# Feed-forward input products as seven half-size products for eight, with weight sums on GpSimd

## The chip, the cores and the metric
One core of a Trainium2 chip runs the whole program in one launch. The metric is the device time in microseconds (us), the median of repeated runs. TensorE multiplies; VectorE (DVE in the rows), ScalarE (ACT) and GpSimd (POOL) do the elementwise work; SyncE (SP) issues the transfers from HBM. Each engine works through its own queue in order, and waits at an instruction whose input is not there.

## The reference
A trunk of two layers on a sequence of 512 tokens with 1024 features, in float32. Each layer has a mixer (layer 0: HGRN2 and stick-breaking heads, layer 1: mLSTM heads) and a feed-forward part, both conditioned on a vector c. The feed-forward part is what the change touches:
```
def modulate(x, g, shift, scale):
    return (rmsnorm(x, g) * (1.0 + scale) + shift)

def conv_glu_ffn(h, w_in, conv_w, conv_b, w_out):
    u = jnp.matmul(h, w_in)                 # 512 x 1024 by 1024 x 5632
    a, g = jnp.split(u, 2, axis=-1)         # 2816 features each
    a = causal_dwconv(a, conv_w, conv_b)    # 3 taps along the tokens
    return jnp.matmul(jax.nn.gelu(a) * g, w_out)

x = x + g_f * conv_glu_ffn(modulate(x, norm_ffn_g, sh_f, sc_f), ...)
```
The six shifts, scales and gates of a layer come from `silu(c) @ ada_w + ada_b`, a vector of 6144 per layer.

## The kernel before
Activations are held with features on the 128 partitions and tokens along the row: a tile is 128 features by 512 tokens. Products run in a three-term form: every operand is split into a rounded part (hi) and its rest (lo), and `mm3` (L188) issues hi·hi, lo·hi and hi·lo.

The feed-forward input has 22 tiles of `a` and 22 of `g`. Two tiles of each make a pair of tiles (`fi` is the first tile's number). For a pair, `load_split` (L166) fetches 1024 rows by 256 columns of the `a` weights and as much of the `g` weights into raw buffers of 2048 per partition; ScalarE casts them to hi (L177), VectorE subtracts to lo (L178). `mms` (L1001) then runs 8 x 3 products of 512 columns per tile, 96 a pair. As soon as a tile of `a` is in PSUM, `act_a` (L985) makes the convolution: ScalarE the newest tap with the bias (L988), VectorE two more (L990, L992). When the tile of `g` is there too, `act_g` (L996) takes gelu on ScalarE (L997), multiplies by `g` (L998) and splits into `acth` (L184) and `actl` (L185) on VectorE. The first pair of a layer, `first_half` (L1005), runs in two halves of the tokens, since the second half of h comes later.

Output products: tiles are taken in groups of 8, 8 and 6; behind each of the first two groups 4 blocks of output weights are multiplied with the group's activations and added to x (L314), the third goes through `halves_out` (L316), one token half after the other, which also prepares the next norm.

Conditioning runs beside it: `ada_chunk` (L118) fetches 512 KB of `ada_w` into one of three `ada` buffers four times and accumulates 8 products on VectorE (L129, L131), and `ada_close` (L140) transposes on TensorE, reduces (L147) and adds (L149). A *step* is one fetch with its two products. `take` (L980) runs 5 steps per pair in layer 0 and 3 in layer 1; layer 0's feed-forward part carries the chunks `(0, 10..11)` and `(1, 0..9)`, layer 1's carries its last two.

The order of instructions on each engine is set by the program's order and a scheduler that moves an instruction up where its inputs and buffers allow; the buffers of a pool are handed out in turn, and a new user waits for the last one's readers. `work` has 45 buffers of 520 floats, weights have raw and hi/lo pools of their own.

Of the kernel before, what the change touches and what calls it, by code (L numbers as in the profile page):

```python
# [38 lines left out]
def trunk(ctx: ExitStack, tc: tile.TileContext, xT, par_d, masks_d, ada_w, even_w_in, even_w_out,  # L39
          odd_w_in, odd_w_out, ffn_w_in, ffn_w_out, outT):  # L40
    nc = tc.nc
    NW, NR, NS, NA = 45, 2, 3, 3
# [4 lines left out]
    wsp = ctx.enter_context(tc.tile_pool(name="wsp", bufs=NS))  # L47
# [69 lines left out]
    # ---------------- conditioning  # L117
# [47 lines left out]
    # ---------------- weights and dense products  # L165
    def load_split(srcs, kn, cols, name="w", pool_lo=False):  # L166
        n = kn * cols
        raw = rawp.tile([P, 2048], F32, tag="raw", name=nm(name + "raw"))[:, :n]
        hi = wsp.tile([P, 2048], F32R, tag="wh", name=nm(name + "h"))[:, :n]
        lo = wsp.tile([P, 2048], F32R, tag="wl", name=nm(name + "l"))[:, :n]  # L170
# [6 lines left out]
        nc.scalar.copy(hi, raw)  # L177
        (nc.gpsimd if pool_lo else nc.vector).tensor_sub(lo, raw, hi.bitcast(F32))  # L178
        return hi.rearrange("p (k c) -> p k c", k=kn), lo.rearrange("p (k c) -> p k c", k=kn)
# [13 lines left out]
    def fm_piece(w, c0, h, sink, tiles=2, halves=False):  # L193
        wh, wl = load_split([w[:, c0:c0 + tiles * P]], KD, tiles * P)
        pss = [ps_acc() for _ in range(tiles)] if halves else None
        if halves:
            for hf in range(2):
                ts = slice(hf * 256, hf * 256 + 256)
                for s in range(tiles):
                    sl = slice(s * P, (s + 1) * P)  # L200
                    for k in range(KD):
                        mm3(pss[s][:, ts], wh[:, k, sl], wl[:, k, sl], h[k][0][:, ts], h[k][1][:, ts],
                            k == 0, k == KD - 1)
# [4 lines left out]
        for s in range(tiles):  # L208
            ps = ps_acc()
            sl = slice(s * P, (s + 1) * P)  # L210
            for k in range(KD):
                mm3(ps, wh[:, k, sl], wl[:, k, sl], h[k][0], h[k][1], k == 0, k == KD - 1)
                yield 1
            sink(s, ps)

    def tm_block(w, c0, h, sink):
        a = load_split([w[0:512, c0:c0 + 512]], 4, 512)
        b = load_split([w[512:1024, c0:c0 + 512]], 4, 512)
        for t in range(NCH):
            ps = ps_acc()  # L220
            ts = slice(t * P, (t + 1) * P)
            for k in range(KD):
                wh, wl = a if k < 4 else b
                ah, al = h[k]
                nc.tensor.matmul(ps, ah[:, ts], wh[:, k % 4, :], start=(k == 0), stop=False)  # L225
                nc.tensor.matmul(ps, ah[:, ts], wl[:, k % 4, :], start=False, stop=False)  # L226
                nc.tensor.matmul(ps, al[:, ts], wh[:, k % 4, :], start=False, stop=(k == KD - 1))  # L227
# [3 lines left out]
    # ---------------- norms, on token ranges  # L231
# [45 lines left out]
    class Handoff:  # L277
        """Carries x, updated token half by token half, into the next modulated input h."""
# [37 lines left out]
    def halves_out(w, row0, kn, acts, layer, which, hand, i0, i1, ksplit=None):  # L316
        """Output projection over kn row tiles of w, token half by token half."""
# [5 lines left out]
        for hf in range(2):  # L323
            st = hand.st[hf] = Stat(hf * 256, 256, hand.last and hf == 1)
            done = 0
            for cb in (range(n) if hf == 0 else reversed(range(n))):
                if hf == 0 or cb + 3 < n:
                    held[cb] = load_split([w[row0:row0 + kn * P, cb * cols:(cb + 1) * cols]], kn, cols)
                wh, wl = held[cb]
# [4 lines left out]
                for ks_ in ranges:  # L334
                    for s in range(nb):
# [4 lines left out]
                        for k in ks_:  # L340
                            mm3(ps, wh[:, k, cl], wl[:, k, cl], acts[k][0][:, st.sl], acts[k][1][:, st.sl],
                                k == 0, k == kn - 1)
# [10 lines left out]
    def partial_out(w, row0, kn, acts, layer, which):  # L353
        for cb in range(2):
            wh, wl = load_split([w[row0:row0 + kn * P, cb * 512:(cb + 1) * 512]], kn, 512)
            for s in range(4):
                ps = ps_acc()
                cl = slice(s * P, (s + 1) * P)
                for k in range(kn):
                    mm3(ps, wh[:, k, cl], wl[:, k, cl], acts[k][0], acts[k][1], k == 0, k == kn - 1)  # L360
# [3 lines left out]
    def head_rstd(ops_list, scales=None):  # L364
        """1 / sqrt(sum of squares + P * EPS) of each row; the gains carry the missing sqrt(P)."""
# [12 lines left out]
    def weave(chains, cover, width=2):  # L378
        """Runs up to `width` chains step by step, with products of `cover` between the steps."""
# [20 lines left out]
    # ---------------- HGRN2 head  # L400
    def hgrn_head(hd, q, Q, f, k, va, sgs, out):
# [9 lines left out]
        for l in range(LEVELS):  # L411
# [14 lines left out]
            pn = small.tile([P, 256], F32, tag="pb", name=nm("pb"))  # L426
# [53 lines left out]
    # ---------------- stick-breaking head  # L480
# [41 lines left out]
    # ---------------- even mixer  # L522
    def even_layer():
# [15 lines left out]
        # first block, a quarter of the features at a time, as their conditioning arrives  # L539
        ws = {}  # L540

        def w_load(q):
            rows = slice(q * 256, q * 256 + 256)
            ws[q] = load_split([w[rows, 3072:3584], w[rows, 2560:2816]], 2, 768, pool_lo=True)
# [29 lines left out]
        def products(q, ps_):  # L574
            wh, wl = ws[q]
            for i in range(6):
                for kq in range(2):
# [3 lines left out]
                    wt_ = wl if ps_ == 2 else wh  # L581
# [549 lines left out]
```

## Time and profile before
| | |
|---|---|
| median of 3 runs | 1318.6 us (1317.66 to 1320.1) |
| span of the profiled execution | 1316.1 us |
| TensorE busy | 1271.8 us, 97% |
| VectorE, ScalarE, GpSimd busy | 811.6 (62%), 466.6 (35%), 178.1 us (14%) |
| matmuls | 6458 |
| data moved by DMA | 162.51 MB, mean 123 GB/s |
| feed-forward of layer 0 and 1, the stretches read | 332 to 640 us, 934 to 1270 us |
| odd mixer, the stretch read | 665 to 912 us |

The profiled execution lies 2.5 us below the runs' median, since its span goes from the first to the last instruction. In the rows a matmul's printed duration overlaps the next one's, so the pitch of products is read from start to start. A row's x count is the number of instructions in it.

### The profile page before, as it was taken

To read this page: it belongs to the slowest core of one execution; us is meant where nothing else is said; L and a number is where in the kernel's file an instruction comes from. 1 tells how busy PE (TensorE), PEld (TensorE's weight loads), DVE (VectorE), ACT (ScalarE), POOL (GpSimd) and SP (SyncE) were. 2 spreads that over 40 slices of the span, in tenths; PEclk is the share of its full clock that TensorE was granted. 3 is DMA by queue.
4 is the path that set the end of the run, shared out by engine and by line. 5 is a ranking of instruction groups with operands and counts; after the bars stand their busy time and mean duration, and the time that the engine had idled before them with its cause. 6 is when DMAs were issued, how large, how long until landed. Compare 5 with 4: busy or idle time off the path is not lost.

```text
span 1316.1 us, 16372 instructions
## 1 busy us (share of the span) xinstructions
PE 1271.8 (97%) x6458; PEld 1053.1 (80%) x6458; DVE 811.6 (62%) x1198; ACT 466.6 (35%) x725; POOL 178.1 (14%) x258
## 2 busy tenths in 40 slices
PE   4899999999999999999999999999999999999997
PEld 3677788889888888888898768778988888888887
DVE  6844368996797368835756865666785435443454
ACT  3354313124432123212245674775532213221321
POOL 1322144414000000000031020113300000000012
PEclk9999999999999999999999999999999999999998
DMA  8741143562476247633433312112152222222221
GB/s 261 254 154 64 64 129 125 164 192 97 140 234 203 95 150 233 201 119 113 152 113 97 127 33 96 65 65 65 65 184 88 97 95 96 96 97 96 80 72 65
DMA packets 132717, 162.51 MB, mean 123 GB/s; under 512 B 4896, under 2 KB 102944, under 8 KB 132640
## 3 DMA queue, kind: packets, MB, share of 16 engines
q1 hardware_dynamic: 132640, 161.46, 37.8%
q8 instruction: 51, 0.84, 0.3%
q14 instruction: 26, 0.21, 0.1%
HBM read 159.35 MB, written 2.10 MB: 123 GB/s over the span
## 4 chain that ended last, share of the span: by engine, by line
PE 86%; DVE 5%; issue 4%; POOL 2%; ACT 2%; DMA 1%; SPq 0%; POOLq 0%; DVEq 0%; ACTq 0%
PE acc L189 19%; PE acc L190 19%; PE acc L191 19%; PE mx L189 5%; PE mx L190 5%; PE mx L191 5%; PE mx L418 2%; PE acc L227 1%; PE acc L225 1%; PE acc L226 1%; PE mx L808 1%; PE mx L834 1%; PE mx L463 1%; POOL sqa L247 1%; PE mx L145 1%
## 5 line engine op out<-in xcount | busy, mean ns | idle before, releaser
L190 PE MATMUL acc<-hl,wah 128*128 128x512 f32 (+1 forms) x384 | 144.2, 377 | 1.1 <-DVE hl L310 1.0
L189 PE MATMUL acc<-hh,wah 128*128 128x512 f32 (+1 forms) x384 | 145.0, 378 | 0.0
L191 PE MATMUL acc<-hh,wgl 128*128 128x512 f32 (+1 forms) x384 | 144.3, 376 | 0.0
L191 PE MATMUL acc<-hh,wal 128*128 128x512 f32 (+1 forms) x384 | 144.1, 376 | 0.0
L189 PE MATMUL acc<-hh,wgh 128*128 128x512 f32 (+1 forms) x384 | 144.1, 375 | 0.0
L190 PE MATMUL acc<-hl,wgh 128*128 128x512 f32 (+1 forms) x384 | 144.0, 375 | 0.0
L178 DVE TENSOR_TENSOR wl<-wraw,wh 128x2048 fp32r<-128x2048 f32 (+1 forms) x41 | 89.9, 2192 | 54.2 <-ACT wh L177 54.2
L177 ACT CAST wh<-wraw 128x2048 fp32r<-128x2048 f32 (+1 forms) x45 | 79.8, 1774 | 104.5 <-PE acc L190 69.7
L189 PE MATMUL acc<-hh,wh 128*128 128x512 f32 x272 | 111.5, 410 | 0.0
L131 DVE SCALAR_TENSOR_TENSOR adaacc<-adaraw,cs,adaacc 128x512 f32<-128x512 f32 x140 | 106.8, 763 | 6.2 <-DMA adaraw<-ada_w 4.2
L190 PE MATMUL acc<-hl,wh 128*128 128x512 f32 x272 | 108.2, 398 | 0.0
L191 PE MATMUL acc<-hh,wl 128*128 128x512 f32 x272 | 108.0, 397 | 0.0
L245 POOL TENSOR_TENSOR sqa<-sq,sq 128x256 f32<-128x256 f32 x8 | 10.9, 1365 | 698.4 <-ACT sq L239 698.4
L190 PE MATMUL mx<-actl,wdh 128*128 128x512 f32 x256 | 101.0, 395 | 0.0
L189 PE MATMUL mx<-acth,wdh 128*128 128x512 f32 x256 | 101.0, 396 | 0.0
L191 PE MATMUL mx<-acth,wdl 128*128 128x512 f32 x256 | 100.9, 394 | 0.0
L177 ACT CAST wgh<-wgraw 128x2048 fp32r<-128x2048 f32 x22 | 42.0, 1908 | 123.6 <-PE acc L190 86.7
L190 PEld LDWEIGHTS acc<-hl,wah 128*128 128x128 f32 x384 | 72.1, 188 | 15.8 <-DVE hl L310 2.0
L190 PEld LDWEIGHTS acc<-hl,wgh 128*128 128x128 f32 x384 | 72.3, 188 | 14.2
L189 PEld LDWEIGHTS acc<-hh,wgh 128*128 128x128 f32 x384 | 72.2, 188 | 14.1
L191 PEld LDWEIGHTS acc<-hh,wgl 128*128 128x128 f32 x384 | 72.1, 188 | 14.0
L191 PEld LDWEIGHTS acc<-hh,wal 128*128 128x128 f32 x384 | 72.1, 188 | 14.0
(267 smaller groups left out, 2686.6 us busy)
## 6 DMA issues: line engine op xcount, KB each, us to landing
adaraw<-ada_w SPq DMA_DIRECT2D x80, 512.0 KB, 4.4
waraw<-ffn_w_in SPq DMA_DIRECT2D x22, 1024.0 KB, 5.1
wgraw<-ffn_w_in SPq DMA_DIRECT2D x22, 1024.0 KB, 5.1
wdraw<-ffn_w_out SPq DMA_DIRECT2D x16, 1024.0 KB, 4.9
wraw<-odd_w_in SPq DMA_DIRECT2D x12, 1024.0 KB, 5.1
wraw<-even_w_in SPq DMA_DIRECT2D x11, 1024.0 KB, 5.1
adaraw<-ada_w SPq DMA_DIRECT2D x32, 256.0 KB, 4.3
wraw<-ffn_w_out SPq DMA_DIRECT2D x10, 768.0 KB, 4.2
```

Source lines behind the costliest of these rows:

```text
L131: nc.vector.scalar_tensor_tensor(a, r[:, i2, :], cs[:, k:k + 1], a, op0=ALU.mult, op1=ALU.add)
L145: nc.tensor.transpose(ps[:, j * P:(j + 1) * P], a[:, j * P:(j + 1) * P], ident)
L177: nc.scalar.copy(hi, raw)
L178: (nc.gpsimd if pool_lo else nc.vector).tensor_sub(lo, raw, hi.bitcast(F32))
L189: nc.tensor.matmul(out, ah, bh, start=start, stop=False)
L190: nc.tensor.matmul(out, ah, bl, start=False, stop=False)
L191: nc.tensor.matmul(out, al, bh, start=False, stop=stop)
L225: nc.tensor.matmul(ps, ah[:, ts], wh[:, k % 4, :], start=(k == 0), stop=False)
L226: nc.tensor.matmul(ps, ah[:, ts], wl[:, k % 4, :], start=False, stop=False)
L227: nc.tensor.matmul(ps, al[:, ts], wh[:, k % 4, :], start=False, stop=(k == KD - 1))
L247: nc.gpsimd.tensor_add(self.acc, self.acc, s)
L418: nc.tensor.matmul(lps[:, c * 64:(c + 1) * 64].rearrange("p (b m) -> p b m", m=m), k[:, s], qu, start=True, stop=True)
```

## The change
Feed-forward input products of all pairs but the first of each layer go by Strassen's scheme in Winograd's form. A block of 256 weight columns, 1024 rows, is a 2 x 2 grid of quarters (512 rows by 128 columns), and h a grid of (512 features by 256 tokens). Seven products of quarters, of sums of weight quarters and of sums of h quarters, take the place of eight. Each of the seven is 12 products of 256 columns (4 feature tiles, 3 terms); the seven are X1 to X7 for the `a` block and Y1 to Y7 for the `g` block.

- The h sums are made once per layer, behind the first pair (L1159 to L1180): VectorE subtracts, ScalarE casts, VectorE makes the lows. `modulate` keeps the unsplit h in `hf` tiles, where GpSimd adds the shift.
- The weight sums are made for each block on GpSimd, four of 128x512 (`Seven.sum`, L1055), and then split by `split_w` (L196, L197).
- A job's product lands in PSUM; ScalarE copies four of a block's results away (L1092, L1094, L1097, L1107), VectorE adds three (L1100, L1103, L1105). X6, X7 and X4 add onto what X1 left in the same bank, X3 onto X5's.
- Both tiles' activation stands in `post`, at the end of a pair's 14 jobs. The hi cast of the activation is on ScalarE (L1136, before VectorE's L184).
- Jobs are emitted with weights fetched 16 jobs and prepared 6 jobs ahead.
- One pool of 72 buffers of 520 floats takes what `work` and the hi/lo pools were; raw buffers are 6 of 1024 floats in place of 2 of 2048, `ada` buffers 2 in place of 3. All weights are split in pieces of 512 per partition (they were 2048, 1536 in places).
- Output groups are 6, 6, 6 and 4 tiles. `take` runs 6 steps behind `fi` = 2 and 4 (and before the pair's activation), then 2. Six chunks of layer 1's conditioning, 4 to 9, go from layer 0's feed-forward part to the odd mixer, with one in front of some of its projections.

```
-    NW, NR, NS, NA = 45, 2, 3, 3
+    NW, NR, NA = 72, 6, 2
...
+    def split_w(src, name, view=None, pool_lo=False):
+        hi = wt(name + "h", dt=F32R)[:, :512]
+        lo = wt(name + "l", dt=F32R)[:, :512]
...
+        nc.scalar.copy(h, src)
+        (nc.gpsimd if pool_lo else nc.vector).tensor_sub(l, src, h.bitcast(F32))
...
+            if t1s is not None:
+                nc.gpsimd.tensor_scalar(t1, t1, sh, 0.0, op0=ALU.add, op1=ALU.add)
...
         def cover():
+            yield from ada_many(1, (4,))
             yield from fm_piece(w, 2048, h, og_sink(0))
+            yield from ada_many(1, (5,))
...
+    ORDER = ("X1", "X5", "Y1", "Y5", "X6", "Y6", "X2", "X7", "Y2", "Y7", "X3", "X4", "Y3", "Y4")
+    LEAD, FETCH = 6, 16
...
+        def sum(self, a, b, op):
+            s = wt("ws", [P, 4, P])
+            nc.gpsimd.tensor_tensor(s, a, b, op=op)
+            return s
...
+            elif n == 5:
+                src = self.s1 = self.sum(self.q(1, 0), self.q(1, 1), ALU.add)
+            elif n == 6:
+                src = self.s2 = self.sum(self.s1, self.q(0, 0), ALU.subtract)
...
+            for kk in range(4):
+                ks = slice(kk * P, (kk + 1) * P)
+                bh, bl = self.bs[n][kk]
+                nc.tensor.matmul(ps, hi[:, ks], bh, start=first and kk == 0, stop=False, skip_group_check=True)
+                nc.tensor.matmul(ps, hi[:, ks], bl, start=False, stop=False, skip_group_check=True)
+                nc.tensor.matmul(ps, lo[:, ks], bh, start=False, stop=kk == 3, skip_group_check=True)
+            a = self.ps["a"]
+            if n == 1:
+                self.p = wt("pp", [P, 2, 256])
+                nc.scalar.copy(self.p[:, 0, :], a)
+            elif n == 5:
+                nc.scalar.copy(self.p[:, 1, :], ps)
+            elif n == 6:
+                self.u2 = wt("u2")[:, :256]
+                nc.scalar.copy(self.u2, a)
+            elif n == 2:
+                self.v[0] = wt("v")
+                nc.vector.tensor_add(self.v[0][:, 0:256], ps, self.p[:, 0, :])
...
-        groups = ((0, 8), (8, 8), (16, 6))
+        groups = ((0, 6), (6, 6), (12, 6), (18, 4))
...
+        for kk in range(4):
...
+            nc.vector.tensor_sub(u[:, 0, :], b12, b11)
+            nc.vector.tensor_sub(v[:, 0, :], b22, b12)
+            nc.vector.tensor_sub(u[:, 1, :], b22, u[:, 0, :])
+            nc.vector.tensor_sub(v[:, 1, :], b21, u[:, 1, :])
+            for t, ns in ((u, (5, 6)), (v, (7, 4))):
+                hi = wt("th", [P, 2, 256], dt=F32R)
+                lo = wt("tl", [P, 2, 256], dt=F32R)
+                nc.scalar.copy(hi, t)
+                nc.vector.tensor_sub(lo, t, hi.bitcast(F32))
...
+            def post(gi):
+                take(6 if fi < 6 else 2)
+                for s in range(2):
+                    acts_of.setdefault(gi, []).append(act_g(act_a(fi + s, blocks["X"].v[s]), blocks["Y"].v[s]))
...
+        for j, (_, _, run, post) in enumerate(jobs):
+            while nf < min(j + FETCH, len(jobs)):
+                if jobs[nf][0]:
+                    jobs[nf][0]()
+                nf += 1
+            while npr < min(j + LEAD, len(jobs)):
+                jobs[npr][1]()
+                npr += 1
+            run()
+            if post:
+                post()
...
     def side0():
         yield from ada_many(0, (10, 11))
-        yield from ada_many(1, range(10))
+        yield from ada_many(1, range(4))
```
How the instructions stand now is seen at two places, the end of a pair and the start of the feed-forward part. ScalarE in the kernel before, early in layer 0's feed-forward part: `wah`, `wgh` and `wdh` are weight pieces, `cv` a tile in convolution and gelu.
```order
L997 ACT_TABLE_LOAD
L997 ACTIVATE cv_2949<-cv_2949 128x512
L177 CAST wgh_2998<-wgraw_2997 128x2048
L988 ACTIVATE cv_2959<-acc_2713,par 128x512
L177 CAST wah_3152<-waraw_3151 128x2048
L997 ACTIVATE cv_2959<-cv_2959 128x512
L988 ACTIVATE cv_3028<-acc_3003,par 128x512
L177 CAST wgh_3158<-wgraw_3157 128x2048
L997 ACTIVATE cv_3028<-cv_3028 128x512
L177 CAST wah_3312<-waraw_3311 128x2048
```
The two steps of a tile lie between single weight casts. VectorE at the same place of the kernel before: `wal`, `wgl` are the weights' lows, `adaraw` the conditioning.
```order
L990 SCALAR_TENSOR_TENSOR cv_3028<-acc_3003,par,cv_3028 128x511
L131 SCALAR_TENSOR_TENSOR adaacc_2986<-adaraw_3123,cs,adaacc_2986 128x512
L992 SCALAR_TENSOR_TENSOR cv_3028<-acc_3003,par,cv_3028 128x510
L131 SCALAR_TENSOR_TENSOR adaacc_2986<-adaraw_3123,cs,adaacc_2986 128x512
L131 SCALAR_TENSOR_TENSOR adaacc_2986<-adaraw_3127,cs,adaacc_2986 128x512
L178 TENSOR_TENSOR wgl_3159<-wgraw_3157,wgh_3158 128x2048
L998 TENSOR_TENSOR cv_3028<-cv_3028,acc_3032 128x512
L131 SCALAR_TENSOR_TENSOR adaacc_2986<-adaraw_3127,cs,adaacc_2986 128x512
L184 CAST acth_3059<-cv_3028 128x512
L131 SCALAR_TENSOR_TENSOR adaacc_2986<-adaraw_3131,cs,adaacc_2986 128x512
L185 TENSOR_TENSOR actl_3060<-cv_3028,acth_3059 128x512
```
Taps, gate and splits of a tile are mixed with conditioning and weight lows. VectorE in the changed kernel at the start of layer 0's feed-forward part, the last of four like quarters of the h sums: `tu` and `tv` are the sums, `tl` their lows, `wal` and `wgl` the lows of the first weight pieces of X and Y.
```order
L1164 TENSOR_TENSOR tu_3314<-hf_2868 128x256
L1165 TENSOR_TENSOR tv_3315<-hf_2892,hf_2868 128x256
L1166 TENSOR_TENSOR tu_3314<-hf_2892,tu_3314 128x256
L1167 TENSOR_TENSOR tv_3315<-hf_2892,tu_3314 128x256
L1172 TENSOR_TENSOR tl_3321<-tu_3314,th_3320 128x512
L1172 TENSOR_TENSOR tl_3325<-tv_3315,th_3324 128x512
L197 TENSOR_TENSOR wal_3341<-waraw_3328,wah_3340 128x512
L197 TENSOR_TENSOR wal_3347<-ws_3344,wah_3346 128x512
L197 TENSOR_TENSOR wgl_3351<-wgraw_3332,wgh_3350 128x512
```
The first weight piece comes behind all four quarters. VectorE in the changed kernel behind the first pair of seven (`fi` = 2) of layer 0: `adaraw` and `adaacc` are conditioning, `cv` the tile, `v` what the jobs left.
```order
L197 TENSOR_TENSOR wal_3626<-ws_3623,wah_3625 128x512
L128 TENSOR_SCALAR adaacc_3642<-adaraw_3643,cs 128x512
L130 SCALAR_TENSOR_TENSOR adaacc_3642<-adaraw_3643,cs,adaacc_3642 128x512
L130 SCALAR_TENSOR_TENSOR adaacc_3642<-adaraw_3647,cs,adaacc_3642 128x512 x2
L130 SCALAR_TENSOR_TENSOR adaacc_3642<-adaraw_3651,cs,adaacc_3642 128x512 x2
L130 SCALAR_TENSOR_TENSOR adaacc_3642<-adaraw_3655,cs,adaacc_3642 128x512 x2
L128 TENSOR_SCALAR adaacc_3659<-adaraw_3660,cs 128x512
L130 SCALAR_TENSOR_TENSOR adaacc_3659<-adaraw_3660,cs,adaacc_3659 128x512
L1125 SCALAR_TENSOR_TENSOR cv_3668<-v_3505,par,cv_3668 128x511
L130 SCALAR_TENSOR_TENSOR adaacc_3659<-adaraw_3664,cs,adaacc_3659 128x512
L1127 SCALAR_TENSOR_TENSOR cv_3668<-v_3505,par,cv_3668 128x510
L130 SCALAR_TENSOR_TENSOR adaacc_3659<-adaraw_3664,cs,adaacc_3659 128x512
```
Conditioning stands ahead of the first tile's taps and between them. ScalarE in the changed kernel at the end of a pair in layer 0 and the start of the next: `v` the tiles of X and Y, `acth` the activation's hi, `pp` the copy of the next pair's X1.
```order
L196 CAST wah_4811<-ws_4809 128x512
L1123 ACTIVATE cv_4843<-v_4691,par 128x512
L1107 COPY v_4748<-acc_4601 128x256
L1132 ACTIVATE cv_4843<-cv_4843 128x512
L1136 CAST acth_4849<-cv_4843 128x512
L1123 ACTIVATE cv_4853<-v_4711,par 128x512
L1132 ACTIVATE cv_4853<-cv_4853 128x512
L1136 CAST acth_4859<-cv_4853 128x512
L196 CAST wgh_4869<-ws_4867 128x512
L1092 COPY pp_4886<-acc_4873 128x256
L196 CAST wah_4892<-waraw_4502 128x512
L1094 COPY pp_4886<-acc_4896 128x256
```
The two tiles' activation is now one stretch, and the next pair's copies (`pp`) stand behind it.

## Rows read from the trace of the kernel before

**Rows 1.** The page, section 1 and section 4, first line: busy, and chain.
```profile
PE 1271.8 (97%) x6458; PEld 1053.1 (80%) x6458; DVE 811.6 (62%) x1198; ACT 466.6 (35%) x725; POOL 178.1 (14%) x258
...
PE 86%; DVE 5%; issue 4%; POOL 2%; ACT 2%; DMA 1%; SPq 0%; POOLq 0%; DVEq 0%; ACTq 0%
```

**Rows 2.** Table by stretch: length, then engines' busy us, clock, DMA share, GB/s.
```profile
332.00:640.00 308.00, 308.00 (x1400) 252.19 (x1399) 209.14 (x268) 81.48 (x73) 0.00 (x0) 1.00 0.53 170
665.00:912.00 247.00, 242.99 (x1274) 196.93 (x1274) 158.19 (x296) 148.24 (x288) 48.73 (x92) 1.00 0.24 79
934.00:1270.00 336.00, 335.85 (x1542) 275.42 (x1541) 170.73 (x200) 91.40 (x91) 4.43 (x3) 1.00 0.30 98
```

**Rows 3.** Timeline of TensorE, end of layer 1's input products: start, us, engine, line.
```profile
1259.18 0.40 PE L189 MATMUL acc<-hh,wah 128*128 128x512 f32 x1
...
1270.33 0.28 PE L189 MATMUL acc<-acth,wh 128*128 128x256 f32 x1
...
1272.10 0.28 PE L189 MATMUL acc<-acth,wh 128*128 128x256 f32 x1
```

**Rows 4.** Groups by form: count, busy us, mean ns, idle time before.
```profile
L177 ACT CAST wgh<-wgraw 128x2048 fp32r<-128x2048 f32 x22 | 42.0, 1908 | 123.6 <-PE acc L190 86.7 <-PE mx L190 36.9
L177 ACT CAST wh<-wraw 128x1536 fp32r<-128x1536 f32 x14 | 20.7, 1479 | 43.1 <-PE acc L190 21.8 <-DMA wraw<-even_w_in 21.1
L445 ACT COPY off<-mx 128x256 f32<-128x256 f32 x4 | 1.5, 370 | 10.5 <-PE mx L438 10.5
...
L131 DVE SCALAR_TENSOR_TENSOR adaacc<-adaraw,cs,adaacc 128x512 f32<-128x512 f32 x140 | 106.8, 763 | 6.2 <-DMA adaraw<-ada_w 4.2
L185 DVE TENSOR_TENSOR actl<-cv,acth 128x512 fp32r<-128x512 f32 x44 | 30.4, 691 | 1.2
L147 DVE TENSOR_REDUCE mod<-mx 128x4 f32<-128x512 f32 x20 | 13.5, 686 | 3.9 <-PE mx L145 3.9
L163 DVE SCALAR_TENSOR_TENSOR affA<-mod,par 128x2 f32<-128x2 f32 x4 | 8.2, 2056 | 0.0
L500 DVE TENSOR_TENSOR be<-be,pr 128x256 f32<-128x256 f32 x4 | 1.8, 440 | 0.0
```

**Rows 5.** Timelines of VectorE and ScalarE, handoffs within one tile's activation.
```profile
1142.99 0.75 DVE L990 SCALAR_TENSOR_TENSOR cv<-acc,par,cv 128x511 f32<-128x511 f32 x1 [0.60 <-ACT cv L988]
1143.78 0.75 DVE L992 SCALAR_TENSOR_TENSOR cv<-acc,par,cv 128x510 f32<-128x510 f32 x1
...
1142.18 0.78 ACT L988 ACTIVATE cv<-acc,par 128x512 f32<-128x512 f32 x1 [3.36 <-PE acc L191]
1144.62 0.63 ACT L997 ACTIVATE cv<-cv 128x512 f32<-128x512 f32 x1 [1.66 <-DVE cv L992]
```

**Rows 6.** The page, section 6: DMA issues, median us to landing.
```profile
adaraw<-ada_w SPq DMA_DIRECT2D x80, 512.0 KB, 4.4
```

**Rows 7.** Timelines of GpSimd and VectorE where they meet; L245's group.
```profile
1276.83 1.99 POOL L245 TENSOR_TENSOR sqa<-sq,sq 128x256 f32<-128x256 f32 x1 [334.48 <-ACT sq L239]
1279.27 0.74 POOL L247 TENSOR_TENSOR sqa<-sqa,sq 128x256 f32<-128x256 f32 x1 [0.46 <-ACT sq L239]
...
1276.47 1.76 DVE L178 TENSOR_TENSOR wl<-wraw,wh 128x1536 fp32r<-128x1536 f32 x1 [0.91 <-ACT wh L177]
...
22.54 3.44 POOL L178 TENSOR_TENSOR wl<-wraw,wh 128x1536 fp32r<-128x1536 f32 x1 [6.47 <-ACT wh L177]
...
23.28 3.25 DVE L562 SCALAR_TENSOR_TENSOR qa<-adaraw,cs,qa 128x512 f32<-128x512 f32 x1 [0.82 <-ACT qa L560]
...
27.11 0.74 DVE L562 SCALAR_TENSOR_TENSOR qa<-adaraw,cs,qa 128x512 f32<-128x512 f32 x1
...
L245 POOL TENSOR_TENSOR sqa<-sq,sq 128x256 f32<-128x256 f32 x8 | 10.9, 1365 | 698.4 <-ACT sq L239 698.4
```

**Rows 8.** Table by stretch, the program's start and end; columns as in rows 2.
```profile
0.00:10.00 10.00, 0.00 (x0) 0.00 (x0) 3.13 (x7) 5.53 (x9) 1.25 (x10) 1.00 0.83 264
...
1312.00:1316.10 4.10, 0.00 (x0) 0.00 (x0) 0.93 (x3) 0.00 (x0) 0.00 (x0) 0.50 0.65 217
```

More of the change, by code (lines that the diff above doesn't have):

```diff
@@ L163, in make_affine, with __init__, get, load_raw @@
         nc.vector.scalar_tensor_tensor(affA[:, i, j0:j0 + n], mod[:, o:o + n], 1.0, g, op0=ALU.add, op1=ALU.mult)
[L166 to L170, printed above, removed]
+    class Weights:
+        def __init__(self, ku, cw, pieces):
+            self.ku, self.cw, self.pieces = ku, cw, pieces
+        def get(self, k, cl):
+            hi, lo = self.pieces[k // self.ku]
+            o = k % self.ku * self.cw
+            cl = slice(o + cl.start, o + cl.stop)
+            return hi[:, cl], lo[:, cl]
+    def load_raw(srcs, kn, cols, name):
+        raw = rawp.tile([P, 1024], F32, tag="raw", name=nm(name + "raw"))[:, :kn * cols]
         r3 = raw.rearrange("p (k c) -> p k c", k=kn)
@@ L542, in w_load @@
         def w_load(q):
-            rows = slice(q * 256, q * 256 + 256)
-            ws[q] = load_split([w[rows, 3072:3584], w[rows, 2560:2816]], 2, 768, pool_lo=True)
+            rows = [slice(q * 256 + i * P, q * 256 + (i + 1) * P) for i in range(2)]
+            ws[q] = []
+            for r in rows:
+                raw = load_raw([w[r, 3072:3584], w[r, 2560:2816]], 1, 768, "w")
+                ws[q].append((split_w(raw[:, 0:512], "w", pool_lo=True), split_w(raw[:, 512:768], "w", pool_lo=True)))
         aq = {}
@@ L709, in odd_gates @@
             for k in range(KD):
-                nc.tensor.matmul(gps, gw[:, k, :], h[k][part], start=(part == k == 0),
+                nc.tensor.matmul(gps, gws[k // 4][:, k % 4, :], h[k][part], start=(part == k == 0),
                                  stop=(part == 1 and k == KD - 1))
@@ L998, in act_g @@
             nc.vector.tensor_mul(c0t, c0t, gps)
[L999 to L1003 removed]
+            hi = wt("acth", dt=F32R)
+            lo = wt("actl", dt=F32R)
+            nc.scalar.copy(hi, c0t)
+            nc.vector.tensor_sub(lo, c0t, hi.bitcast(F32))
+            return hi, lo
         def first_half(pss, wa, wg):
@@ L1041, in ffn, with out_jobs, fetch, prep @@
+        def out_jobs(gi):
+            f0, fn = groups[gi]
+            for cb in range(4):
+                st = {}
+                def fetch(cb=cb, st=st):
+                    st["raw"] = load_raws([wd[f0 * P:(f0 + fn) * P, cb * 256:(cb + 1) * 256]], fn, 256, "wd")
+                def prep(st=st):
+                    st["w"] = load_split(None, fn, 256, "wd", raws=st["raw"])
+                def run(cb=cb, st=st):
                     for s in range(2):
@@ L1044, in ffn @@
                         for k in range(fn):
-                            mm3(ps, wo[0][:, k, sl], wo[1][:, k, sl], acts[k][0], acts[k][1], k == 0, k == fn - 1)
+                            mm3(ps, *st["w"].get(k, sl), *acts_of[gi][k], k == 0, k == fn - 1)
                         x_update(ps, layer, 1, cb * 2 + s)
-            else:
-                drain(side)
-                ada_close()
-                drain(halves_out(wd, f0 * P, fn, acts, layer, 1, out, 0, 2))
+                jobs.append((fetch, prep, run, None))
+        for fi in range(2, NF, 2):
+            set_jobs(fi)
+            if fi in (4, 10, 16):
+                out_jobs(fi // 6)
+        nf = npr = 0
+        for j, (_, _, run, post) in enumerate(jobs):
[9 more added lines that the diff above has]
+                post()
+        drain(side)
+        ada_close()
+        drain(halves_out(wd, 18 * P, 4, acts_of[3], layer, 1, out, 0, 2))
     HG_STEP, SB_STEP, ML_STEP, HG_T, SB_T, ML_T, ML_A = 2, 2, 3, 5, 2, 3, 4
```

204 lines of the change are left out of this document (134 added, 70 removed).

## The prediction
> **What bounds the kernel now.** I read the page's busy shares first, then the chain that ended last, then a table by stage. TensorE is busy 97% of the span, and 86% of the chain is TensorE work [rows 1]. In the two feed-forward stretches, 332–640 and 934–1270 us, it works without a gap at granted clock 1.00, the upper level of 2.4 GHz, with VectorE busy 209 of 308 and 171 of 336 us, ScalarE 81 and 91, GpSimd 0 and 4 [rows 2]. So every product removed there is worth its pitch at once, and every wait put in front of a product costs its full length.
>
> **The products removed, A.** The profiled execution has a span of 1316.1 us; the runs lie at 1317.66 to 1320.1, median 1318.6, so 2.5 us lie around the span, and I add changes to 1318.6. In layer 1's last pair 48 products of 512 columns start from 1259.18 until the next kind starts at 1270.33: 0.2323 us each [rows 3]. The 15 of 256 columns behind them start from 1270.33 until 1272.10: 0.118 each. A pair before costs 96 x 0.2323 = 22.30 us; after, it is 14 jobs of 12 products of 256 columns, 168 x 0.118 = 19.82. Ten pairs a layer change (the first keeps whole products): 20 x 2.48 = **-49.6**.
>
> **Start of the feed-forward, B.** VectorE forms the factor sums between the first pair's activation and X1's weight piece (VectorE's first piece in the changed kernel: the last of four like quarters of L1164 to L1172, then `wal_3341`). One quarter is four subtractions of 128x256 at 0.44, two lows of 512 at 0.69 and three links of 0.06 (they run 0.03 to 0.09 in the handoffs shown): 3.3, four are 13.3 [rows 4, 5]. The first pair's own lows take 2.0 before them, and X1's low 0.69 behind. TensorE has run all it had by then: its next product is X1. So 16 us a layer, two layers **+32**; ends 25 (the sums of 12.6 alone) and 40 (4.1 more, one tile's activation, in front).
>
> **End of a pair, C.** Before, a tile's activation stands beside the next tile's products (ScalarE's piece of before), and nobody waits. After, both tiles' activations stand at the pair's end, and in ScalarE's queue the copy of the next X1 (`pp_4886<-acc_4873`) is behind them (ScalarE's piece of the changed kernel). X6 adds into the bank of X1, so it may not start before that copy. One tile's chain: ScalarE 0.63, VectorE 0.75 and 0.75 (taps), ScalarE 0.63 (gelu), VectorE 0.69 (gate, two tensors of 512 as in L185), ScalarE 0.62 (cast; the line through 1.479 at 1536 and 1.908 at 2048, at 512), 4.07 in all, and a low of 0.69 beside the next step [rows 4, 5]. I take L997's 0.63 for the first step too, which now reads SBUF (its end from PSUM is L988's 0.78). Two tiles are 8.1 and ten links 0.5; the first step and part of the first tap run before Y4 ends: the last cast is done 8.0 us behind it. A weight cast (0.62) and the copy (0.37) later X6 may go, at 9.0. TensorE has X1, X5, Y1 and Y5 to run, 4 x 12 x 0.118 = 5.66. That leaves 3.3 at X6 and 0.6 more at Y6: 3.9 a boundary. Six of a layer's boundaries lead to a pair (behind fi = 2, 6, 8, 12, 14, 18); behind 4, 10 and 16 come output products, up to 53 of them at 0.232 in front of what needs the last tile, which cover the chain. Layer 1: 5 x 3.9 = 19.5. Layer 0 has conditioning as well: 2 x 4.6 (a reduce, 0.69), 6.0 (a reduce and L163, 2.06, of it 1.4 in the way), 2 x 8.3 (four conditioning steps on two buffers: one more landing of 4.4 us) [rows 4, 6]. Behind fi = 2 there are eight steps, ahead of the taps and between them (VectorE's second piece). A step gives its buffer free after two products of 0.76 and the next lands 4.4 later, 5.9 a round; three rounds and 1.5 put the eighth at 19.2; two products with a tap between, gate and cast, 3.6, and the taps that the earlier steps let in, 0.75, put the last cast at 23.6. 23.6 + 1.0 + 0.6 - 5.66 = 19.4 in each layer. Sum: 19.5 + 9.2 + 6.0 + 16.6 + 38.8 = **+90**. Ends: 50 (the steps done early, all twelve at 3.9 or 4.6) and 100 (0.15 on each first step, two more links).
>
> **Smaller terms.** Output products behind fi = 4 and 10 of layer 0 meet four steps: 0 to one landing, 4.4; I take 2.7, so D = +5.4. At the end of each layer the last output weights' casts stand behind the last activation, with no product to cover them: 8.0 + 0.62, less 1.4 as the first tile is a job earlier there, 7.2, so E = +14.4 (ends 0 and 17). The odd mixer takes six conditioning chunks of 8 x 0.76: 36.5 us more VectorE where it has 158 of 247 [rows 2]. 195 is no bound, but heads wait for VectorE in turn: 0 to +30, I take +5.
>
> **GpSimd's sums beside VectorE, F.** Each pair gives GpSimd eight sums of 128x512, a form that no row has. A sum of 256 alone takes 0.74; one that began beside a VectorE subtraction took 1.99, done 0.6 behind that one's end; and a VectorE step of 0.74 that met a GpSimd subtraction of 1536 took 3.25 [rows 7]. So each holds the other up to its end. For 512 I take 1.28, the line through 0.74 at 256 and 3.44 at 1536 (ends 1.15, a third of 3.44, and 2.7, twice L245's mean). A pair has 10.2 us of sums, and of VectorE's two-tensor work 14 x 0.69 + 2 x (1.5 + 0.69 + 0.69) = 15.4: 25.6 in sequence against 19.82 + 3.9 = 23.7 of TensorE time. 1.9 over, in 18 pairs **+34**. Ends: 0, if the sums fall where such work is absent; 92, if at each boundary four of the chain's steps meet a sum (5.1).
> The Trainium skill, page "SBUF — State Buffer", section "Who interferes with whom", says that VectorE and GpSimd share a pair of ports as an exclusive lock, and that a VectorE instruction with two SBUF inputs and a GpSimd instruction that reads SBUF block each other for the whole instruction; the trace agrees (3.25 against 0.74, 1.99 against 0.74). The rule speaks against this change: by it the sum is the one here, without it 34 less.
>
> **The clock.** Behind the program's last products, while TensorE waits, the granted clock is 0.50, the lower level; in the first 10 us, before its first product, it reads 1.00 [rows 8]. After the four long waits (16 and 19 us) some products may run at the lower level: 0 to +16 in all, I take +8.
>
> **Sum.** 1318.6 - 49.6 + 32 + 90 + 5.4 + 14.4 + 5 + 34 + 8 = **1458 us**.
>
> **Rivals.**
> Light: F is nothing, 1424. For it: VectorE is busy in only 0.51 to 0.68 of the stretches, so sums find room; against it, both meetings shown held the later one up fully.
> Heavy: the boundary's chain meets sums, F is 92: 1516. For it: preparation runs six jobs ahead, so the next pair's sums are due just there; against: the queue of sums may be done before.
> Other side, not slower: nothing waits for the activation at a pair's end. If the last cast lies within 4.7 us of Y4 (5.66 less 0.99), C, D, F, the mixers' term and the clock fall out: 1318.6 - 49.6 + 32 + 14.4 = 1315. The two tiles' chains would have to overlap almost wholly; the order has them one behind the other on both queues, and one alone is 4.07.
> The change doesn't do what it says: if a product of 256 columns has a pitch of 22.30 / 168 = 0.133 or more, since its weight load takes longer than its columns, A is gone: 1508. For it: the load unit is busy 80% even so [rows 1]; against: fifteen products at 0.118.
>
> **Chances and range.** Forecast 0.49, light 0.20, heavy 0.16, other side 0.10, no saving 0.05. The range goes from 1370 (light, with C at 50, and mixers and clock at nothing: 1371) to 1520 (just over heavy). The measurement can tell 0.2%, 2.6 us, from no change; the other side lies at that edge, so 0.07 faster, 0.03 the same, 0.90 slower.
>
> **What would show it.** Right: products of 256 columns at 0.118; TensorE waits at X6 and Y6 of nearly every pair, released by ScalarE's copies (L1092); a wait of about 16 us ahead of the first X1 and of about 19 ahead of the X6 behind fi = 2; VectorE's subtractions of 512 longer than 0.69 where GpSimd works. Wrong: TensorE without these waits, or waits on weight pieces in the middle of a pair (then six jobs ahead are too few, and not the activation counts), or on raw weights from DMA.

## The result, and the profile after
The changed kernel takes 1597.9 us (1596.25 to 1600.18, four runs) against 1318.9 before: ratio 1.2121, 95% interval 1.21 to 1.2142. It is 279 us slower; the forecast was 1458, slower by 139, with a range to 1520. The profiled execution has a span of 1598.5 us against 1316.1.

The page's busy shares of the changed kernel answer [rows 1]:
```profile
PE 1312.0 (82%) x7802; PEld 1148.3 (72%) x7802; DVE 1052.4 (66%) x1750; ACT 643.0 (40%) x1364; POOL 433.8 (27%) x462
```
TensorE is busy 40 us longer though its products are cheaper by 49.6, and 286.5 us of the span are without a product, 44.3 before.

The same table by stage, of the kernel before and then of the changed one; a line is: length, then busy us of PE, PEld, DVE, ACT, POOL, granted clock, DMA share, GB/s. The five stages are everything up to the first feed-forward product, layer 0's feed-forward products, the time to layer 1's first, those, and the rest. Before:
```profile
0.00:317.45 317.45, 287.07 (x1522) 236.45 (x1523) 212.79 (x332) 108.51 (x212) 94.65 (x131) 0.99 0.46 150
317.45:658.84 341.39, 340.74 (x1593) 280.69 (x1592) 231.25 (x305) 93.30 (x93) 5.28 (x5) 1.00 0.51 165
658.84:932.08 273.24, 269.20 (x1493) 222.93 (x1492) 174.28 (x322) 160.10 (x310) 59.36 (x104) 1.00 0.24 79
932.08:1270.33 338.25, 337.60 (x1553) 276.85 (x1551) 172.65 (x203) 93.52 (x93) 5.29 (x5) 1.00 0.31 100
1270.33:1316.10 45.77, 37.18 (x305) 36.17 (x303) 20.64 (x38) 11.20 (x21) 13.50 (x15) 0.92 0.22 74
```
After:
```profile
0.00:370.36 370.36, 304.55 (x1523) 245.78 (x1523) 213.96 (x385) 112.65 (x272) 100.07 (x147) 0.94 0.41 127
370.36:801.93 431.57, 348.74 (x2335) 323.76 (x2335) 317.54 (x461) 177.87 (x353) 134.85 (x97) 0.90 0.34 105
801.93:1141.70 339.77, 283.84 (x1420) 229.35 (x1420) 209.82 (x447) 163.89 (x365) 57.77 (x108) 0.89 0.30 93
1141.70:1562.68 420.98, 347.98 (x2318) 323.39 (x2319) 292.36 (x420) 177.89 (x353) 130.16 (x97) 0.89 0.27 83
1562.68:1598.50 35.82, 26.88 (x208) 25.97 (x208) 18.70 (x41) 10.67 (x25) 10.96 (x15) 0.88 0.18 59
```
The last output group has 4 tiles in place of 6, so 96 products of 256 columns, 11.3 us, move per layer from the stage behind into the feed-forward part. With that set right the feed-forward parts lose 150 us (90.2 + 82.7 - 22.6) and the mixers 131 (52.9 + 66.5 + 11.3). Counted the other way: products -49.6; TensorE without a product +242.2 (35.4, 82.2, 51.9, 72.3 and 0.4 by stage); products slower by 89.8 in all (1312.0 less 1271.8 - 49.6). The sum is 282.4, the difference of the spans.

The waits of TensorE in the changed kernel (what it waited for, us in total, times, longest):
```profile
PE acc L1086 <- ACT pp L1092: 92.6, 12, 19.9
PE acc L225 <- ACT wh L196: 37.5, 12, 8.4
PE acc L1086 <- ACT wah L196: 34.5, 2, 17.2
...
PE acc L227 <- DVE wl L197: 11.4, 7, 5.4
PE mx L144 <- DVE adaacc L130: 10.0, 1, 10.0
```
The first and third are the pair ends and the starts of the forecast. Of the second, 11.9 are the ends of the two layers (term E); its other 25.6 and the fourth are the mixers' weight pieces, which had no term. The fifth is conditioning. Further down the list stand waits on other tiles of the odd mixer (`mb`, 13.5 in all, and `stk`, 6.9), which were hardly there before (0.2).

One pair end in layer 1, the table by stretch (columns as above) and then TensorE's timeline (start, us, line, wait before it):
```profile
1342.00:1346.00 4.00, 2.27 (x20) 2.06 (x18) 2.55 (x4) 1.97 (x3) 1.28 (x1) 1.00 0.00 0
1346.00:1350.00 4.00, 0.00 (x0) 0.00 (x0) 2.52 (x5) 2.01 (x5) 0.00 (x0) 0.66 0.00 0
1350.00:1354.00 4.00, 3.92 (x18) 3.92 (x19) 3.36 (x6) 3.82 (x10) 0.00 (x0) 0.50 0.00 0
1354.00:1358.00 4.00, 4.00 (x35) 4.00 (x34) 2.43 (x5) 2.99 (x7) 0.00 (x0) 0.98 0.07 7
```
```profile
1338.07 0.28 PE L1086 MATMUL acc<-th,wgh 128*128 128x256 f32 x1
...
1339.85 0.28 PE L1086 MATMUL acc<-th,wah 128*128 128x256 f32 x1
...
1350.08 0.58 PE L1086 MATMUL acc<-th,wah 128*128 128x256 f32 x1 [5.81 <-ACT pp L1092]
1350.46 0.42 PE L1087 MATMUL acc<-tl,wah 128*128 128x256 f32 x1
...
1353.88 0.40 PE L1088 MATMUL acc<-th,wgl 128*128 128x256 f32 x1
```
Fifteen products from 1338.07 to 1339.85 are 0.118 apart, as in [rows 3]. Behind the wait of 5.8 us the clock is at 0.50 and the pitch 0.214 (16 products from 1350.46 to 1353.88) for about 4 us.

### The profile page after: what moved, and what is told of

Same layout as the page of the kernel before. It is cut to its first block, busy times and chain, and to the rows that moved or that the text cites. A ratio compares the mean times of both kernels' runs of the same rounds, so it can differ in the third digit from the quotient of the medians.

```text
span 1598.5 us, 20947 instructions
## 1 busy us (share of the span) xinstructions
PE 1312.0 (82%) x7802; PEld 1148.3 (72%) x7802; DVE 1052.4 (66%) x1750; ACT 643.0 (40%) x1364; POOL 433.8 (27%) x462
## 5 line engine op out<-in xcount | busy, mean ns | idle before, releaser
L1086 PE MATMUL acc<-th,wah 128*128 128x256 f32 x320 | 99.3, 310 | 92.6 <-ACT pp L1092 92.6
L1086 PEld LDWEIGHTS acc<-th,wah 128*128 128x128 f32 x320 | 67.7, 212 | 95.0 <-ACT pp L1092 95.0
L197 DVE TENSOR_TENSOR wl<-wraw,wh 128x512 fp32r<-128x512 f32 x140 | 91.9, 693 | 17.8 <-ACT wh L196 17.8
L1087 PE MATMUL acc<-tl,wah 128*128 128x256 f32 x320 | 97.4, 304 | 0.0
L1088 PE MATMUL acc<-th,wal 128*128 128x256 f32 x320 | 97.4, 304 | 0.0
L1086 PE MATMUL acc<-th,wgh 128*128 128x256 f32 x320 | 93.4, 292 | 0.0
L1087 PE MATMUL acc<-tl,wgh 128*128 128x256 f32 x320 | 92.8, 290 | 0.0
L1088 PE MATMUL acc<-th,wgl 128*128 128x256 f32 x320 | 92.4, 289 | 0.0
L1055 POOL TENSOR_TENSOR ws<-waraw,waraw 128x512 f32<-128x512 f32 x20 | 28.6, 1430 | 222.6 <-PE mx L226 117.4
L196 ACT CAST wh<-wraw 128x512 fp32r<-128x512 f32 (+1 forms) x156 | 83.5, 608 | 4.3 <-DMA wraw<-even_w_in 4.2
L197 DVE TENSOR_TENSOR wal<-ws,wah 128x512 fp32r<-128x512 f32 x80 | 74.1, 926 | 13.6 <-ACT wah L196 12.5
L197 DVE TENSOR_TENSOR wal<-waraw,wah 128x512 fp32r<-128x512 f32 x68 | 57.7, 851 | 33.6 <-ACT wah L196 33.3
```

The lines of the kernel that those rows point to most:

```text
L196: nc.scalar.copy(h, src)
L197: (nc.gpsimd if pool_lo else nc.vector).tensor_sub(l, src, h.bitcast(F32))
L1055: nc.gpsimd.tensor_tensor(s, a, b, op=op)
L1086: nc.tensor.matmul(ps, hi[:, ks], bh, start=first and kk == 0, stop=False, skip_group_check=True)
L1087: nc.tensor.matmul(ps, hi[:, ks], bl, start=False, stop=False, skip_group_check=True)
L1088: nc.tensor.matmul(ps, lo[:, ks], bh, start=False, stop=kk == 3, skip_group_check=True)
```

## Experiments
Times are medians, of two runs each unless said; the kernel before, run beside them, took 1316.9 to 1317.7 us.

**The changed pools without the seven products.** The feed-forward part of before, the rest as changed:
```
-    ORDER = ("X1", "X5", ...)   # and class Seven, set_jobs, out_jobs
+            mms(aps, wa, sl, full)      # 512 columns, as before
+    self.t1s = None
```


> The changed kernel with the feed-forward part of before (products of 512 columns, no sums, groups 8, 8, 6), on the changed pools, weight pieces of 512 and conditioning order. Theory one pool: the mixers lose by themselves, since weights share the one pool of 72 buffers and are no longer prepared a piece ahead: stage up to the feed-forward part of layer 0 stays near 370 us (317 before), the odd mixer's stage near 350 (273 before), the feed-forward parts return to about 341 and 338; span about 1316 + 53 + 78 = 1447 us. Rival, that the mixers are slow only through what the seven products leave behind (buffers, queue positions): both mixer stages come back to 317 and 273, span about 1320 to 1350.


Measured 1542.4 us. The mixers' stages stay at 371.3 and 353.5 us, as the first theory said; the feed-forward parts, which it put at 341 and 338, took 393 and 374. So 225 us of loss come without one of the seven products:
```profile
PE acc L227 <- DVE wal L197: 39.5, 16, 3.4
PE acc L225 <- ACT wh L196: 31.4, 11, 8.5
```
These two longest are waits on weight pieces, and so are two of the next three (16.2 and 13.9); the other is on conditioning (21.7).

**The same with the weights in a pool of their own.**
```
-    NW, NR, NA = 72, 6, 2
+    NW, NR, NA, NS = 46, 6, 2, 13
-        hi = wt(name + "h", dt=F32R)[:, :512]
+        hi = wsp.tile([P, 512], F32R, tag="wh", name=nm(name + "h"))     # lo: tag "wl"
```


> As the kernel with ordinary products on the changed pools, but weight pieces have a pool of their own again (13 hi and 13 lo buffers of 512, 46 for the rest; 72 in all as before). Theory one pool: the waits of TensorE on weight casts (L196) go from some 50 us to under 10, stage up to the feed-forward part about 325 us, odd mixer about 290 (its conditioning is still there), span about 1335. Rival, that the pieces of 512 or the two conditioning buffers do it: nothing changes, span about 1447.


Measured 1337.0 us, 205 less from that edit. The stages are those of before but for the odd mixer and 9 us in the first:
```profile
0.00:326.20 326.20, 289.09 (x1522) 238.25 (x1523) 214.25 (x385) 119.93 (x278) 91.36 (x144) 0.98 0.47 150
326.20:667.54 341.34, 339.34 (x1568) 278.38 (x1567) 206.99 (x336) 112.81 (x185) 3.96 (x4) 1.00 0.41 129
667.54:952.54 285.00, 274.99 (x1517) 225.97 (x1516) 208.26 (x444) 168.53 (x368) 55.36 (x105) 0.99 0.38 119
```
What the one pool does is seen in ScalarE's timeline of the changed kernel, at a piece of the even mixer:
```profile
187.04 0.60 ACT L677 ACTIVATE f<-acc 128x512 f32<-128x512 f32 x1 [4.35 <-PE acc L227]
187.53 0.59 ACT L678 ACTIVATE k<-acc 128x512 f32<-128x512 f32 x1
188.01 2.18 ACT L196 CAST wh<-wraw 128x512 fp32r<-128x512 f32 x4
```
and at the same place with the weights' own pool:
```profile
168.37 0.60 ACT L678 ACTIVATE f<-acc 128x512 f32<-128x512 f32 x1 [4.51 <-PE acc L228]
168.87 0.59 ACT L679 ACTIVATE k<-acc 128x512 f32<-128x512 f32 x1
169.47 0.62 ACT L197 CAST wh<-wraw 128x512 fp32r<-128x512 f32 x1
170.84 0.62 ACT L197 CAST wh<-wraw 128x512 fp32r<-128x512 f32 x1 [0.75 <-PE acc L227]
...
174.15 0.59 ACT L678 ACTIVATE f<-acc 128x512 f32<-128x512 f32 x1
```
With one pool the four casts of the next piece come behind the last copy out of PSUM of the piece before, when TensorE has nothing left (it waits 2.0 us there); with their own they come ahead of the last two copies (from 174.15), one by one, and TensorE doesn't wait.

**Fewer buffers in the one pool.**
```
-    NW, NR, NA = 72, 6, 2
+    NW, NR, NA = 56, 6, 2
```


> The kernel with ordinary products on one shared pool (1542 us), with 56 buffers in that pool in place of 72. Theory that buffers are given out in the order of the program, so that a weight cast cannot pass the tiles asked for ahead of it however many buffers are free: the same time, 1530 to 1555 us. Rival, that 72 buffers are too few for weights and the rest together: with 16 fewer the waits on weight casts grow, 1580 us or more.


Measured 1539.2 us, no slower than with 72. So the number of buffers is not what is short. That a weight piece doesn't get one ahead of the tiles asked for earlier in the program fits this and the order of the casts above; it is argued, not tested by itself.

**Conditioning back, on own pools.** The six chunks in layer 0's feed-forward part again, three conditioning buffers (12 + 12 for weights, 45 for the rest).
```
-            yield from ada_many(1, (4,))      # to 9, in the odd mixer's cover
+        yield from ada_many(1, range(10))     # side0
```


> The kernel with ordinary products on own pools (1337 us), with six chunks of conditioning back in layer 0's feed-forward part, three conditioning buffers, 12 hi and 12 lo weight buffers and 45 for the rest. Theory that the conditioning's place is what is left of the loss: odd mixer's stage from 285 back to about 275, the first stage from 326 to about 319, 1318 to 1323 us. Rival, that the pieces of 512 (four casts and lows for one) are what is left: 1335 to 1340.


Measured 1321.3 us (eight runs), ratio 1.0033 (1.002 to 1.0047). So 16 of the 20 us left are the conditioning and its buffers, 9 of them in the odd mixer's stage, and pieces of 512 cost 4 us at most.

**Filler where TensorE waits, in the changed kernel.**
```
+        fills = {0: 140, 18: 150}     # and 30 ahead of the other X6 behind a pair
+            for i in range(n):
+                nc.tensor.matmul(ps[:, :256], h[0][0][0][:, 0:P], h[0][0][0], start=i == 0, stop=i == n - 1)
```


> The changed kernel with products that nobody reads put on TensorE just where it waits: 140 of 256 columns ahead of the first X1 of a layer, 150 ahead of the X6 behind fi = 2, 30 ahead of the X6 at the other ends of pairs that another pair follows. They do no useful work. Theory of the clock: the waits are filled, TensorE's clock stays at 1.00 there and the products behind run at 0.118 in place of 0.213, 30 to 45 us less in all: 1555 to 1570 us. Rival, that the clock falls for another reason or the half speed costs nothing (the products behind it wait anyway): 1595 or more.


Measured 1574.6 us, 23 less, though TensorE does 880 products more. The granted clock of the feed-forward parts goes from 0.90 and 0.89 to 0.98 and 0.97:
```profile
370.21:793.09 422.88, 389.24 (x2775) 364.23 (x2775) 316.70 (x461) 177.38 (x353) 133.92 (x97) 0.98 0.35 108
1130.75:1540.58 409.83, 388.96 (x2759) 364.03 (x2759) 293.57 (x420) 177.19 (x353) 130.31 (x97) 0.97 0.27 86
```
So the clock falls where TensorE waits, and half speed is paid. The amount is under my 30 to 45; some waits were longer than the filler (7.2 and 4.8 us are left behind it), which accounts for a part at least.

**The pair's activation spread.**
```
-                    acts_of.setdefault(gi, []).append(act_g(act_a(fi + s, ...), ...))
+                later.extend([lambda: taps(0), lambda: gate(0), lambda: taps(1), lambda: gate(1),
+                              lambda: take(6 if fi < 6 else 2)])     # one behind jobs 2, 4, 5, 6, 8
```


> The changed kernel with the activation of a pair put in four parts behind jobs 2, 4, 5 and 6 of the next pair, and the conditioning steps behind them. Theory of the queue (pair end): TensorE's waits at X6 on ScalarE's pp copies, 92.6 us, go to under 15, and some 25 us of half-speed products behind them, so 1480 to 1500 us. Rival, that VectorE and GpSimd together cannot serve a pair in 19.8 us (25.6 us in sequence): the waits come back inside the pair on weight pieces or copies, a pair stays near 25 us, 1540 to 1580.


Measured 1559.3 us: 39 less, in the range of the rival. No wait on a `pp` copy is left, but new ones stand inside the pairs, as the rival said:
```profile
PE mx L144 <- DVE adaacc L130: 23.9, 5, 10.1
PE acc L1088 <- DVE wgl L197: 15.8, 12, 2.5
PE acc L1086 <- DVE v L1103: 15.1, 2, 7.6
```
All three end on VectorE.

**First jobs ahead of the factor sums.**
```
+        FIRST = ("X1", "Y1", "X2", "Y2", "X5", "Y5", "X6", "Y6", "X7", "Y7", "X3", "X4", "Y3", "Y4")
+        while npr < 4: ...        # fetch and prepare these before the sums
```


> The changed kernel with the weights of the layer's first four jobs prepared ahead of the factor sums and these jobs being the ones that need no sums (X1, Y1, X2, Y2; then X5, Y5, X6, Y6, X7, Y7, X3, X4, Y3, Y4). Theory of the start: the wait of 17.2 us ahead of X1 goes, four jobs (5.7 us) run beside the sums and 8 to 11 us remain ahead of X5; with less at half speed 12 to 20 us less in all, 1578 to 1586. Rival, that X1 waits for the first pair's activation or for banks and not for the sums: 1595 or more.


Measured 1591.2 us, 7 less, between the two theories: a miss. In each layer X1 waits 3.1 us and X5 9.8, 12.9 in place of 17.2. So X1 did wait for the sums, but most of the wait only moves. With all repairs (below) X1 has no such wait, and 16.1 us come at X5.

**Seven products on own pools.**
```
+    NW, NR, NA, NS = 52, 6, 2, 10
```


> The changed kernel with seven products, but weight pieces in a pool of their own (10 hi and 10 lo buffers of 512, 52 for the rest, 72 in all); up to nine pieces prepared ahead. Theory that the parts add up: mixers as in the kernel with ordinary products on own pools (326 and 274), the feed-forward parts as in the changed kernel (432 and 421), tail 36: 1489 us, 110 less than the changed kernel. Rival, that the seven products' own buffers are short too and the pools' price in the feed-forward part is part of the 173 us there: 1430 to 1460. Other rival: 52 buffers are too few for the sums, 1510 or more.


Weights get the pool `wsp` as above, and in the feed-forward part no more than nine pieces are prepared ahead, so that the ten buffers do. Measured 1481.2 us: 117 less, the sum of the parts to 8 us. Mixers 325.4 and 282.4, feed-forward parts 423.8 and 414.5: the mixers, which the limit of nine doesn't touch, get back 102 us, the feed-forward parts 14. So the pool's price in the changed kernel lies in the mixers. The waits on `mb` and `stk` go too (0.7 and 0.2 are left): the one pool had held up more than the weight pieces.

**All three repairs, and the same without GpSimd's sums.**
```
-            nc.gpsimd.tensor_tensor(s, a, b, op=op)
-            return s
+            return a
```


> Seven products with weights in their own pool, the pair's activation in four parts behind jobs of the next pair, and the first jobs ahead of the factor sums: all three repairs. Theory that the parts add up: 1489 less 41 (activation, as it gave) less 16 (start) = 1432 us. Theory that VectorE and GpSimd in sequence (25.6 us a pair) are then the bound: a pair near 25 us where TensorE needs 19.8, 1420 to 1460; without that bound the feed-forward parts could come to 345 and the time to 1310 to 1340.

> As the kernel with all three repairs, but GpSimd's weight sums are left out (a quarter of the weights stands in for each sum, so the output is not the reference's). Theory of the port: without the sums VectorE's steps are not held up, a pair falls from about 25 us to near 20, and 18 pairs give 60 to 90 us less than the kernel with all three repairs. Rival, that the sums cost nothing on the path: within 10 us of it.


In the second a quarter of the weights stands in for each sum. Measured 1450.4 and 1384.0 us. The first lies in the second theory's range and 18 above the first's: the waits on conditioning sums (L145 <- adaacc), 10.0 in the changed kernel, are 44.8 now. The sums cost 66 us. How is seen in the former at a layer's start, VectorE and then GpSimd:
```profile
1048.45 0.42 DVE L1235 TENSOR_TENSOR tv<-hf,hf 128x256 f32<-128x256 f32 x1
1048.79 1.51 DVE L1236 TENSOR_TENSOR tu<-hf,tu 128x256 f32<-128x256 f32 x1
1050.34 0.43 DVE L1237 TENSOR_TENSOR tv<-hf,tu 128x256 f32<-128x256 f32 x1
1050.99 1.73 DVE L1242 TENSOR_TENSOR tl<-tu,th 128x512 fp32r<-128x512 f32 x1 [0.22 <-ACT th L1241]
```
```profile
1048.63 1.39 POOL L1056 TENSOR_TENSOR ws<-ws,waraw 128x512 f32<-128x512 f32 x1 [2.30 <-DVE tu L1234]
1050.91 1.26 POOL L1056 TENSOR_TENSOR ws<-ws,wgraw 128x512 f32<-128x512 f32 x1 [0.89 <-DVE tv L1237]
```
A subtraction of 0.42 took 1.51, a low of 0.68 took 1.73, each beside a sum that had begun just before, and was done 0.3 and 0.6 behind that sum's end.

**The sums left out of the changed kernel alone** (same edit).


> The changed kernel with GpSimd's weight sums left out (a quarter of the weights stands in for each sum, so the output is not the reference's) and nothing else changed. The forecast's term for the port: 34 us less (its ends 0 and 92). Theory that the waits of this kernel cover most of the port's price: the wait ahead of X1 falls from 17.2 to about 13.5 and the waits at X6 from 5.8 to 3.9 where a sum had met the chain, 15 to 30 us less in all, against 66 us with all three repairs.


Measured 1520.0 us (1515 to 1525), 78 less, more than either theory. The feed-forward parts, by stage:
```profile
362.33:755.47 393.14, 339.39 (x2335) 317.05 (x2335) 271.81 (x461) 176.92 (x353) 19.02 (x17) 0.93 0.36 116
1092.24:1475.94 383.70, 336.32 (x2318) 314.47 (x2318) 249.89 (x420) 176.64 (x353) 19.12 (x17) 0.94 0.29 91
```
VectorE has as many instructions as with the sums (461 and 420) and is busy 46 and 42 us less: the sums had stretched its steps, whatever else waited for them. The waits at pair ends and starts shrink:
```profile
PE acc L1084 <- ACT pp L1090: 51.7, 12, 15.7
...
PE acc L1084 <- ACT wah L196: 28.1, 2, 14.1
```
41 and 6 us of wait, and with shorter waits less at half speed: products take 21 us less.

**Conditioning spread, and sums on VectorE**, both on top of all three repairs.
```
+            if j % (2 if j < 28 else 6) == 1:
+                take(1)
```
```
-            nc.gpsimd.tensor_tensor(s, a, b, op=op)
+            nc.vector.tensor_tensor(s, a, b, op=op)
```


> The kernel with all three repairs (1450 us), with the conditioning steps one at a time behind every second job (every sixth from the third pair on) and the transposes of a chunk two steps later. Theory of the conditioning wait: the 44.8 us that TensorE waits for the conditioning sums go, 1395 to 1410 us. Theory that VectorE and GpSimd in sequence bound a pair: most of it comes back as waits on weight lows, 1425 to 1450.

> The kernel with all three repairs and spread conditioning, with the weight sums on VectorE in place of GpSimd (eight of 512 a pair, at 0.69 in place of 1.28). Theory of the port as a lock: VectorE has 23.4 us a pair alone where both in sequence had 25.6, so it is as fast or up to 40 us faster than with the sums on GpSimd. Rival, that GpSimd's sums run mostly beside VectorE and hold nothing up: 18 x 5.5 = 100 us slower.


Measured 1417.4 us, between the theories (the waits on conditioning sums go from 44.8 to 1.1, but only 33 us of time), and 1382.7, 35 less: with 160 more instructions, 0.68 us each, VectorE is busy 596 us in the feed-forward parts in place of 603. GpSimd's sums held it up by more than they took off it. The feed-forward parts are 368 and 361 us there, 341 and 338 before plus 11 each for the moved products: even so the seven lose. No version tried beats the kernel before.

## Why the prediction was wrong
**A, the products:** right. The pitch is 0.118 at full clock.

**B, the start:** right in place and size. 17.2 us in each layer where 16 was forecast; 3.1 of it goes with the sums (14.1 without). What X1 waits for last is ScalarE's cast of its weights, which stands behind the casts of the factor sums, and not VectorE's low.

**C, pair ends:** right in place and in the releaser; that the sum agrees (92.6 against 90; 18.6 and 19.9 behind fi = 2 where 19.4 was forecast) is luck, as two errors cancel. Without GpSimd's sums it is 51.7, so chain and links were put 40 us too long, and the port filled them: an ordinary end of layer 1 waits 1.4 to 1.9 without the sums, 3.7 to 5.8 with them, and 3.9 was forecast. Without them the first tile's two taps are done as Y4 ends (one such end of layer 1: at 1274.89, Y4's last product starts at 1274.54); the forecast had only a part of the first before it. The 0.6 at Y6 didn't come. (By its own numbers the end behind fi = 2 comes to 19.5, not 19.4.)

**D and E:** 9.3 us of waits of output products on activations (all groups of both layers) where D was 5.4; 6.0 at the end of each layer where 7.2 was forecast.

**F, the port:** the mechanism was right, the size too small: 34 against 78 in the changed kernel and 66 with the repairs. A sum with nothing on VectorE beside it takes 1.29 to 1.31, as the line said (1.28).
Its price isn't the overrun of a pair's 25.6 us but the steps that a sum holds up, most of them in the chains that TensorE waits for (47 of the 78 are waits at pair ends and starts).

**The step that failed:** "Smaller terms", its last sentences, where the mixers got +5, bounds 0 to +30. They lost 131 us. The term priced only the six conditioning chunks, and these cost about what it said (9 us in the odd mixer's stage, with ordinary products); the cause of the rest wasn't in the sum at all. The change puts all weights into the pool of the other tiles, and the prediction put no price on that in the mixers. The order of the changed kernel would have told it: the casts of each piece of a mixer stand in fours behind the copies of the piece before. Shown by four runs: without the seven products the loss is there (1542), with own pools it goes (1337), with fewer buffers it doesn't grow (1539), and in the changed kernel itself own pools give back 102 of the 131. The other 29 were not taken apart there; with ordinary products conditioning and its buffers were 16 of 20.

**The clock** was the second miss: +8, bounds 0 to +16, where products run 89.8 us slower, 45 in the feed-forward parts and 43 in the mixers. I counted four long waits, though C itself had ten more of 3.9 to 8.3; the changed kernel has 55 of over 1 us. Behind a wait of 3.9 us, the one that ends at 1322.00, the clock is at 0.50 as well:
```profile
1322.00:1326.00 4.00, 4.00 (x18) 4.00 (x19) 3.36 (x6) 3.73 (x9) 0.99 (x1) 0.50 0.00 0
```
The filler shows that it's the waiting. In the whole span 168 us of product time lie where the clock is at 0.50. An estimate from the two pitches (0.118 and 0.214) makes 76 of the 89.8 out of that; the other 14 aren't explained. The Trainium skill, page "TensorE: Matmul & The Clock Gate", section "Part 1: The HAM clock gate (the "warmup" mystery)", says that the clock follows TensorE's recent activity; the trace agrees (0.50 behind a wait of 5.8 us).

Together, feed-forward parts: forecast 134 (every term but the mixers'), measured 150. That is close in part by luck: the waits of TensorE there grew by 155 us where B to F sum to 176, and the products lost 45 to half speed where 8 was forecast for the whole kernel. Mixers: forecast 5, measured 131.

## What to carry to other kernels
When pools are merged, look at the order of every stage that uses them, not at the one the change is for: what was prepared ahead from a pool of its own may fall in line behind the other tiles, and the count of buffers need not matter (56 did as well as 72 here; more than 72 wasn't tried). The waits looked at here (3.9 and 5.8 us) were paid twice, in their length and in products at half speed behind them. GpSimd was no free engine beside a busy VectorE: the sums moved to VectorE, at 0.68 each, were cheaper than at 1.26 or more on GpSimd. And a term that comes out right is no proof: here two wrong parts of a pair's end added up to the forecast.

## What the hardware showed that I had not expected
After a wait of 5.8 us products start 0.214 apart in place of 0.118, for 4 us. VectorE's steps beside a GpSimd sum took as much as 3.6 times as long (1.51 against 0.42). What in a pool's hand-out decides which cast may go ahead isn't shown; the runs tell only that it isn't the count of buffers between 56 and 72.
